# A two-layer decoder trunk: products taken in pairs at five places, and the remaining late transposes moved from TensorE to VectorE's blocks and DMAs

## The chip, the cores and the metric

The kernel runs on one core of one Trainium2 chip. The metric is the device time of one execution in microseconds (us), lower is better. The times shown are medians of several runs; the profile is one execution, with its own time beside them.

The core has five engines that run their own instruction queues in order and wait for each other by semaphores: TensorE (PE in the profile, its weight loads PEld), VectorE (DVE), ScalarE (ACT), GpSimd (POOL) and SyncE (SP). SP issues nearly all DMAs here. Matrix products are accumulated in PSUM, which has 8 banks of 128 x 512 float32; everything else is computed from SBUF, and HBM holds inputs, outputs and scratch.

## The reference

The reference is a trunk of two decoder layers over 256 tokens of width 2048, float32, causal. Layer 0 mixes tokens by softmax attention with 16 heads and a forget gate, layer 1 by a mixture of three dilated windows with 8 heads. Each mixer and each MLP follows an RMSNorm, and each adds into one residual stream.

```
for i in range(2):
    h = rms_norm(x, mix_norm_g[i])
    x = x + (fox_attention(h, ...) if i == 0 else dilated_attention(h, ...))
    h = rms_norm(x, mlp_norm_g[i])
    x = x + (relu(h @ mlp_w_up[i]) ** 2) @ mlp_w_down[i]

# fox_attention, per head: q, k are RMS-normalised per head
s = q @ k.T * dh ** -0.5 + c[q] - c[k]         # c: running sum of log forget gates
o = softmax(causal(s)) @ v                     # then o @ w_out

# dilated_attention, per head: three groups g with dilations r = 1, 4, 16, one shared v
s_g = q_g @ k_g.T * dh ** -0.5 - slope * distance   # only distances that r divides, up to 128 * r
o = softmax over all three groups together, @ v     # then o @ w_out
```

## The kernel before

**Products.** All large products run in float32 by splitting each operand into a rounded high part (`fp32r`) and a rest: high x high, high x low, low x high. Weights come from HBM in tiles of 256 rows by 512 columns (`load`, line 262, 512 KB, five buffers `raw`), in the order of the list `plan` (lines 213 to 241). `split` (line 282) makes the two parts: ScalarE casts the tile to `wh` (line 294), VectorE subtracts to `wl` (line 295; called the cut below), five buffers each.

A product has 512 output columns and 16 steps, one for each 128 rows of the contraction (`KC = 16`); every second step uses up one weight tile and calls `split` for the tile five further on. `product` (line 312) accumulates both 128-token halves in two PSUM banks (`acc`, 4 banks, so two products' worth), with six 128x512 matmuls in a step. `product_transposed` (line 359) is the MLP's up product with the weights stationary and the output transposed; it takes four banks: two of `acc` and two of either `sc` or `tp` (`up_banks`, line 861, alternating). The matmuls of one product follow step by step, and one product follows the other.

**The order of everything else.** The class `Jobs` (line 41) counts steps (`tick`). Chains of other work are generators: `yield 3` waits three steps, `yield key` waits until another chain has set that key, and `need(key)` makes a product wait for its input's key. So the numbers in the yields fix where a chain's instructions stand between the matmuls of the products; a scheduler then orders each engine's queue from that program. `behind(...)` asks that an instruction be put behind another one.

**Stages.** Norm n0 and the input; the first layer's queries, keys, values for four groups j of four heads (three products each, with the heads' attention in between); its output projection, four products; MLP n1 (four blocks of four up products and four down products); the dilated layer, four quarters q4 of three products for queries and keys (one for each dilation) and one for the shared values, with two heads each; its output projection; MLP n3.

**Transposes of the residual stream.** The stream `xt` is held token by token in four chunks of 512 columns. After the last product that adds to chunk n (`add_chain`, line 804), `norm_chain` (line 428) turns that chunk into `hT`, the stationary operand of the next stage, four of its 16 steps. For norms n1, n2, n3, chunks 0 to 2 go by `transposed_by_dma` (line 398): per 128 tokens one VectorE transpose in 32x32 blocks (line 405), four 64 KB DMAs into a scratch tensor in HBM (line 408) and one 256 KB DMA back (line 410), all on SP's queue; then ScalarE and VectorE make the two parts (lines 421, 422). The last chunk goes by eight 128x128 transposes on TensorE (line 440), since its product is the last ahead of the stage: only the 12 steps of chunks 0 to 2 stand between it and its use. Then the squares are summed (line 456) and `rstd` is made; it scales the results of the products, not their input.

**Heads.** `qk_chain` (line 482) takes a product of queries and/or keys: squares on ScalarE (line 488), sums on VectorE (line 492), a power on POOL (line 495), three steps later the scaling (lines 499, 501), VectorE's block transposes (line 533), four writes on SP (line 537) and a read on POOL (line 538) for each half, and after `yield 10` and two times `yield 2` the parts (lines 547 to 556). Two groups, named in `by_engine` (line 480), go by TensorE transposes (line 510) and are done sooner: the last keys of the first layer and the last group of the dilated layer, whose heads the output projection waits for. `v_chain` (line 559) takes the values. `fox_head` (line 699) and `dil_head` (line 750) compute a head: scores on TensorE (lines 708, 614, 617) into `sc` banks (two), mask and maximum on VectorE (716, 719; 763, 769), exponentials on ScalarE, scaling on VectorE (727; 777 to 780), three transposes of the probabilities on TensorE (`p_transposed`, line 588), and products with the values (`pv`, line 580). `gate_chain` (line 636) makes the running sum of the log forget gates; line 678 is its small matmul. `dilation_tables` (line 186) makes the distance tables on VectorE.

Of the kernel before, what the change touches and what calls it, by code (L numbers as in the profile page):

```python
# [17 lines left out]
P = 128  # L18
# [18 lines left out]
W_SUB = 2  # L37
RAW_SUB = 2


# [47 lines left out]
def trunk(ctx: ExitStack, tc, x, fox_w_in, fox_b_f, fox_q_gain, fox_k_gain, fox_w_out, dil_w_in,  # L88
# [126 lines left out]
    def add(w, rows, cols):  # L215

        for r in range(rows[0], rows[1], RAW_SUB * P):
            plan.append((w, r, cols))

    for j in range(4):  # L220
        for part in range(3):
            add(fox_w_in[0], (0, D), [(part * D + j * NC, NC)])
    for n in range(NX):
        add(fox_w_out[0], (0, D), [(n * NC, NC)])

    def add_mlp(l):
        for b in range(4):
            for n in range(4):
                add(mlp_w_up[l], (0, D), [(b * D + n * NC, NC)])
            for n in range(NX):  # L230
                add(mlp_w_down[l], (b * D, (b + 1) * D), [(n * NC, NC)])

    add_mlp(0)
    for q4 in range(4):
        for g in range(3):
            c = g * DH * P + q4 * 2 * P
            add(dil_w_in[0], (0, D), [(c, 2 * P), (3 * DH * P + c, 2 * P)])
        add(dil_w_in[0], (0, D), [(6 * DH * P + q4 * NC, NC)])
    for n in range(NX):
        add(dil_w_out[0], (0, D), [(n * NC, NC)])  # L240
    add_mlp(1)
# [69 lines left out]

    def product(keys, lhs, post):

        acc = [ps_acc.tile([P, NC], F32, tag="acc", name=f"acc{used[0]}_{t}") for t in range(NT)]
        for k in range(KC):
            jobs.need(keys(k))
            i = k % W_SUB
            hi, lo = (in_turn(w[:, i, :]) for w in splits[used[0]])
            ah, al = lhs(k)
            for t in range(NT):  # L320
                tok = slice(t * P, (t + 1) * P)
                first, last = k == 0, k == KC - 1
                nc.tensor.matmul(acc[t], ah[:, tok], hi, start=first, stop=False)  # L323
                nc.tensor.matmul(acc[t], ah[:, tok], lo, start=False, stop=False)  # L324
                issued["product"] = nc.tensor.matmul(acc[t], al[:, tok], hi, start=False, stop=last)  # L325
            if i == W_SUB - 1:
                used[0] += 1
                split()
            jobs.tick()
        jobs.spawn(post(acc))  # L330

    def last_product(keys, lhs, ready):
# [25 lines left out]

    def product_transposed(keys, both, banks, post):


        for k in range(KC):
            jobs.need(keys(k))
            i = k % W_SUB
            hi, lo = splits[used[0]]
            tokens = both(k)
            for b in range(NC // P):
                col = slice(b * P, (b + 1) * P)

                def main(first, last):  # L370
                    issued["product"] = nc.tensor.matmul(  # L371
                        banks[b], hi[:, i, col], in_turn(tokens.rearrange("p x s -> p (x s)"), P // 2), start=first, stop=last)

                def rest():
                    nc.tensor.matmul(banks[b][:, 0:S], lo[:, i, col], in_turn(tokens[:, 0, :], P // 2), start=False, stop=False)  # L375

                if k == 0:
                    main(True, False)
                    rest()
                else:  # L380
                    rest()
                    main(False, k == KC - 1)
            if i == W_SUB - 1:
                used[0] += 1
                split()
            jobs.tick()
        jobs.spawn(post(banks))

# [9 lines left out]
    def transposed_by_dma(tag, col, n):  # L398
# [3 lines left out]
        for t in range(NT):  # L402
# [8 lines left out]
            tiles.append(tile_)  # L411
        yield 7
        for half in range(2):
            pr = n * 2 + half
            both = act.tile([P, 2, 2, S], F32R, tag="hT", name=f"hT_{tag}_{pr}", bufs=KC // 2)
            for i in range(2):
                gc = gain[:, col + pr * 2 + i:col + pr * 2 + i + 1]
                for t in range(NT):
                    src = tiles[t].rearrange("p (i b r) -> p b i r", i=4, b=4)[:, half * 2 + i]
                    hi, lo = (both[:, i, x, t * P:(t + 1) * P].rearrange("p (i r) -> p i r", i=4) for x in range(2))  # L420
                    on_act = nc.scalar.activation(hi, src, AF.Copy, scale=gc)
                    on_dve = nc.vector.scalar_tensor_tensor(lo, src, gc, hi.bitcast(F32), ALU.mult, ALU.subtract)
            issued[tag, pr] = issued[tag] = on_act, on_dve
# [4 lines left out]
    def norm_chain(tag, col, n, ssp, wait, later):  # L428
        yield wait
        if tag != "n0" and n < NX - 1:  # L430
            yield from transposed_by_dma(tag, col, n)
# [46 lines left out]


    by_engine = {("fk", 3), ("dqk", 3, 2)}  # L480

    def qk_chain(acc, tag, key, parts):
# [15 lines left out]
        for t in range(NT):  # L498
# [5 lines left out]
            qn.append(q)  # L504
        if key in by_engine:
            yield 4
            for t in range(NT):
                pt = ps_tp.tile([P, 4, P], F32, tag="tp", name=f"ptq_{key}_{t}")
                for h in range(4):
                    nc.tensor.transpose(pt[:, h, :], qn[t][:, h, :], ident)  # L510
                for c, nh, gcol, (whole, hi, lo) in parts:
                    src = pt[:, c // P:c // P + nh, :]
                    gc = gain[:, gcol:gcol + 1]
                    keys = hi.shape[2] == S
                    if t == 0:
                        nc.scalar.activation(whole, src, AF.Copy, scale=gc)
                        if not keys:
                            continue
                    at = slice(t * P, (t + 1) * P) if keys else slice(0, P)
                    for i in range(nh):  # L520

                        order = [x.rearrange("p (h n) -> p h n", h=2) for x in (hi[:, i, at], lo[:, i, at])]
                        of = src[:, i, :].rearrange("p (n h) -> p h n" if keys else "p (h n) -> p h n", h=2)
                        nc.scalar.activation(order[0], of, AF.Copy, scale=gc)
                        nc.vector.scalar_tensor_tensor(order[1], of, gc, order[0].bitcast(F32), ALU.mult, ALU.subtract)
                yield 1
            jobs.done.add(key)
            return

# [106 lines left out]
    def gate_chain(tag, pf):  # L636
# [38 lines left out]
        nc.vector.scalar_tensor_tensor(lf, s, -2.0, z, ALU.mult, ALU.add)  # L675
        yield 6
        pc = ps_sc.tile([P, NT, FH], F32, tag="sc", name="pc")
# [21 lines left out]
    def fox_head(j, hh, qT, kT, vt, sel):  # L699
# [4 lines left out]
        yield "mask"  # L704
        yield (2 if ("fk", j) in by_engine else 4) * hh + 2
        ps = ps_sc.tile([P, 512], F32, tag="sc", name=f"sc_f{h}")
# [23 lines left out]
        yield ("fv", j)  # L730
        yield 2
        if ("f", h // 2) not in oT:
# [17 lines left out]
    def dil_head(q4, i, qTs, kTs, vt):  # L750
        h = 2 * q4 + i
        for g in range(3):
            yield ("dqk", q4, g)
        yield (4 if ("dqk", q4, 2) in by_engine else 6) * i + 2
        s = work.tile([P, 3, 3 * P], F32, tag="sd", name=f"sd{h}", bufs=1)
# [34 lines left out]
    def dilated(tag):  # L790
        for q4 in range(4):
            qTs = [heads_pair(f"dqT{q4}_{g}", g, False) for g in range(3)]
            kTs = [heads_pair(f"dkT{q4}_{g}", 3 + g, True) for g in range(3)]
            for g in range(3):
                product(keys_h(tag), lhs_h(tag),
                        lambda acc: qk_chain(acc, tag, ("dqk", q4, g),
                                             [(0, 2, DIL_G + g, qTs[g]), (2 * P, 2, DIL_G + 3 + g, kTs[g])]))
            vt = values(f"dv{q4}")
            for i in range(2):
                jobs.spawn(dil_head(q4, i, qTs, kTs, vt))  # L800
            product(keys_h(tag), lhs_h(tag), lambda acc: v_chain(acc, tag, ("dv", q4), vt))

# [23 lines left out]

    def out_proj(keys, lhs, then=None, ready=None, scale=None):
        for n in range(NX):
            if ready is not None and n == NX - 1:
                last_product(keys, lhs, final_add(n, scale))  # L830
                continue
            product(keys, lhs, lambda acc, n=n: add_chain(acc, n, then, ready, scale))

# [33 lines left out]
    def mlp(tag, **after):  # L867
        for b in range(4):
            key = f"{tag}a{b}"
            aT = {}  # L870
            for n in range(4):
                product_transposed(keys_h(tag), lambda k: hT[tag][k // 2][:, k % 2], up_banks(key, n),
                                   lambda banks, n=n: up_chain(banks, key, n, aT))
            out_proj(lambda k: (key, k // 2),
# [42 lines left out]
    for j in range(4):  # L917
# [12 lines left out]
        for hh in range(4):  # L930
# [4 lines left out]
             lambda k: (oT["f", k // 2][0][:, k % 2, :], oT["f", k // 2][1][:, k % 2, :]),  # L935
             normed("n1", MLP_G))
    jobs.spawn(dilation_tables())
# [3 lines left out]
             lambda k: (oT["d", k // 2][0][:, k % 2, :], oT["d", k // 2][1][:, k % 2, :]),  # L941
             normed("n3", MLP_G + KC))
    mlp("n3", ready=store)
# [31 lines left out]
```

## Time and profile before

| | us |
|---|---|
| median of 3 runs (lowest, highest) | 2167.12 (2166.98, 2168.76) |
| the profiled execution | 2165.63 |
| its span, first to last instruction | 2163.9 |
| TensorE busy | 2151.7 |
| VectorE busy | 1396.2 |
| ScalarE busy | 1109.2 |
| POOL busy | 71.9 |
| span of the output projection of layer 0, about | 310 to 382 |
| MLP n1, about | 382 to 1055 |
| dilated layer, about | 1055 to 1420 |
| its output projection, about | 1420 to 1495 |
| MLP n3, about | 1495 to 2164 |

The granted TensorE clock is 1.0 throughout. The DMA engines are busy 66% of the time on the queue of the weights. In the profile's rows, matmuls are pipelined: the length of one (0.38 us for 128x512) is longer than the distance to the next one's start (0.216 us), and it is the distance that adds up to the span. A row "A <- B: total, times, longest" of the waits says that A's line stood idle until B's line had released it.

### The profile page before, as it was taken

The page shows a single profiled execution, that of the slowest core. Times are in us where ns is not written, and L with a number is a line of the kernel's source. Part 1 is how long each engine was busy: PE and PEld are TensorE (multiplying, and loading weights), DVE is VectorE, ACT ScalarE, POOL GpSimd, SP SyncE. Part 2 cuts the span into 40 slices and gives each one's busy share as a digit, 9 for nine tenths or more (in the row PEclk, how much of TensorE's full clock was granted, in tenths as well). Part 3 has the DMA queues.
Part 4 walks back from the last instruction along what each step waited for, and adds up shares of the span by engine and source line. Part 5 has one row for each costly group of instructions (what it writes and reads, how often), then busy time and mean ns, then how long its engine had stood idle before and what let it go on. Part 6 is the DMA issues. An engine that isn't in the chain of part 4 may idle for free.

```text
span 2163.9 us, 30015 instructions
## 1 busy us (share of the span) xinstructions
PE 2151.7 (99%) x11248; PEld 1917.1 (89%) x11248; DVE 1396.2 (65%) x1847; ACT 1109.2 (51%) x1536; POOL 71.9 (3%) x88
## 2 busy tenths in 40 slices
PE   9999999999999999999999999999999999999999
PEld 7888888998998998998888888888988988988988
DVE  6777796655665565566667777766655655655664
ACT  6565565544444454455555555655544544544442
POOL 1111000000000000000010010000000000000000
PEclk9999999999999999999999999999999999999999
DMA  7676658666666766767686776767666666666764
GB/s 250 220 224 187 223 176 262 200 201 203 202 203 201 201 203 204 200 200 243 216 254 202 243 224 196 238 202 240 203 202 201 201 204 203 199 202 204 202 210 143
DMA packets 285411, 454.11 MB, mean 210 GB/s; under 512 B 21144, under 2 KB 98512, under 8 KB 285264
## 3 DMA queue, kind: packets, MB, share of 16 engines
q1 hardware_dynamic: 281792, 442.08, 65.7%
q0 software_dynamic: 2912, 9.46, 1.2%
q8 instruction: 88, 1.44, 0.3%
q10 hardware_dynamic: 560, 0.66, 0.1%
q14 instruction: 59, 0.48, 0.1%
HBM read 435.86 MB, written 16.25 MB: 209 GB/s over the span
## 4 chain that ended last, share of the span: by engine, by line
PE 97%; DVE 1%; ACT 1%; issue 1%; POOL 0%; DMA 0%; ACTq 0%; POOLq 0%
PE acc L323 21%; PE acc L324 21%; PE acc L325 21%; PE up_n3a_acc L371 5%; PE up_n1a_acc L371 5%; PE up_n3a_sc L371 3%; PE up_n3a_tp L371 3%; PE up_n1a_tp L371 3%; PE up_n1a_sc L371 3%; PE up_n1a_acc L375 3%; PE up_n3a_acc L375 3%; PE up_n1a_sc L375 1%; PE up_n1a_tp L375 1%; PE up_n3a_sc L375 1%; PE up_n3a_tp L375 1%; DVE wl L295 1%
## 5 line engine op out<-in xcount | busy, mean ns | idle before, releaser
L295 DVE TENSOR_TENSOR wl<-raw,wh 128x1024 fp32r<-128x1024 f32 (+1 forms) x801 | 976.6, 1222 | 691.1 <-ACT wh L294 687.9
L294 ACT CAST wh<-raw 128x1024 fp32r<-128x1024 f32 (+1 forms) x801 | 838.5, 1047 | 926.5 <-PE acc L325 590.7
L323 PE MATMUL acc<-wh,hT_n 128*128 128x512 f32 x896 | 343.6, 384 | 0.2 <-ACT wh L294 0.2
L324 PE MATMUL acc<-wl,hT_n 128*128 128x512 f32 x896 | 340.3, 380 | 0.1
L325 PE MATMUL acc<-wh,hT_n 128*128 128x512 f32 x896 | 339.6, 379 | 0.0
L323 PE MATMUL acc<-wh,aTh_n1a 128*128 128x512 f32 x512 | 194.0, 379 | 0.0
L324 PE MATMUL acc<-wl,aTh_n1a 128*128 128x512 f32 x512 | 194.0, 379 | 0.0
L325 PE MATMUL acc<-wh,aTl_n1a 128*128 128x512 f32 x512 | 194.0, 379 | 0.0
L325 PEld LDWEIGHTS acc<-wh,hT_n 128*128 128x128 f32 x896 | 169.6, 189 | 24.1
L323 PEld LDWEIGHTS acc<-wh,hT_n 128*128 128x128 f32 x896 | 169.6, 189 | 22.7 <-ACT wh L294 0.6
L324 PEld LDWEIGHTS acc<-wl,hT_n 128*128 128x128 f32 x896 | 169.9, 190 | 22.2 <-DVE wl L295 0.4
L323 PE MATMUL acc<-wh,aTh_n3a 128*128 128x512 f32 x480 | 181.9, 379 | 0.0
L324 PE MATMUL acc<-wl,aTh_n3a 128*128 128x512 f32 x480 | 181.9, 379 | 0.0
L325 PE MATMUL acc<-wh,aTl_n3a 128*128 128x512 f32 x480 | 181.9, 379 | 0.0
L371 PE MATMUL up_n3a_acc<-hT_n,wh 128*128 128x512 f32 x512 | 181.6, 382 | 0.0
L371 PE MATMUL up_n1a_acc<-hT_n,wh 128*128 128x512 f32 x512 | 181.6, 382 | 0.0
L375 PE MATMUL up_n1a_acc<-hT_n,wl 128*128 128x256 f32 x512 | 139.6, 273 | 0.0
L375 PE MATMUL up_n3a_acc<-hT_n,wl 128*128 128x256 f32 x512 | 139.6, 273 | 0.0
L324 PEld LDWEIGHTS acc<-wl,aTh_n1a 128*128 128x128 f32 x512 | 96.8, 189 | 13.7
L325 PEld LDWEIGHTS acc<-wh,aTl_n1a 128*128 128x128 f32 x512 | 96.8, 189 | 13.7
L323 PEld LDWEIGHTS acc<-wh,aTh_n1a 128*128 128x128 f32 x512 | 96.8, 189 | 13.7
L371 PEld LDWEIGHTS up_n1a_acc<-hT_n,wh 128*128 128x128 f32 x512 | 96.8, 189 | 13.5
(729 smaller groups left out, 3207.0 us busy)
## 6 DMA issues: line engine op xcount, KB each, us to landing
raw<-in_mlp_w_up_dram SPq DMA_DIRECT2D x256, 512.0 KB, 4.0
raw<-in_mlp_w_down_dram SPq DMA_DIRECT2D x256, 512.0 KB, 3.8
raw<-in_dil_w_in_dram SPq DMA_DIRECT2D x192, 256.0 KB, 3.3
raw<-in_fox_w_in_dram SPq DMA_DIRECT2D x95, 512.0 KB, 4.2
raw<-in_fox_w_out_dram SPq DMA_DIRECT2D x32, 512.0 KB, 4.2
raw<-in_dil_w_in_dram SPq DMA_DIRECT2D x32, 512.0 KB, 7.0
raw<-in_dil_w_out_dram SPq DMA_DIRECT2D x32, 512.0 KB, 5.0
blocks_n<-turned_n SPq DMA_DIRECT2D x72, 64.0 KB, 2.1
```

What stands on the lines that cost most here:

```text
L294: issued["cast"] = nc.scalar.copy(hi[:, part, :], raw[:, part, :])
L295: issued["cut"] = nc.vector.tensor_sub(lo[:, part, :], raw[:, part, :], hi[:, part, :].bitcast(F32))
L323: nc.tensor.matmul(acc[t], ah[:, tok], hi, start=first, stop=False)
L324: nc.tensor.matmul(acc[t], ah[:, tok], lo, start=False, stop=False)
L325: issued["product"] = nc.tensor.matmul(acc[t], al[:, tok], hi, start=False, stop=last)
L371: issued["product"] = nc.tensor.matmul(banks[b], hi[:, i, col], in_turn(tokens.rearrange("p x s -> p (x s)"), P // 2), start=first, stop=last)
L375: nc.tensor.matmul(banks[b][:, 0:S], lo[:, i, col], in_turn(tokens[:, 0, :], P // 2), start=False, stop=False)
```

## The change

**Pairs.** At five places two products that follow each other are taken together: the first 12 steps of the first, the first 12 of the second, the last 4 of the first, the last 4 of the second (`CUT = 12`). The places are the first two products of both output projections, the first two up products of both MLPs, and the first two products of the dilated layer. `plan` is reordered in the same way, so the weights come in that order. `product` and `product_transposed` are split into a part that makes the banks and a part that runs given steps.

**Order in the dilated layer.** In the first quarter the values' product comes first, paired with that of the first dilation's heads; then the other two dilations. In the other quarters it stays last.

**Transposes.** The last chunk of n1, n2, n3 goes by `transposed_by_dma` as well, whose wait becomes 9 steps instead of 7 and whose parts are put behind the latest cast and cut; `by_engine` and its branch are gone, so all heads go by blocks and DMAs. n0 keeps TensorE.

**Waits.** In `gate_chain` 10 steps instead of 6 ahead of the running sum; in `fox_head` 3 steps instead of 2 between the transposes of the probabilities and the products with the values; the heads of the last group of the first layer stand 3 steps apart (2 before), the two heads of the last quarter of the dilated layer 6 apart (4 before).

```diff
+    def add_pair(*chunks):
+        for rows in ((0, CUT * P), (CUT * P, D)):
+            for w, cols in chunks:
+                add(w, rows, cols)
...
+    def in_pair(new, steps, posts):
+        banks = []
+        for n in range(2):
+            banks.append(new(n))
+            steps(banks[n], range(CUT))
+        for n in range(2):
+            steps(banks[n], range(CUT, KC))
+            jobs.spawn(posts[n](banks[n]))
...
-        yield 7
+        yield 9
...
-                    on_act = nc.scalar.activation(hi, src, AF.Copy, scale=gc)
-                    on_dve = nc.vector.scalar_tensor_tensor(lo, src, gc, hi.bitcast(F32), ALU.mult, ALU.subtract)
+                    with behind(issued["cast"]):
+                        on_act = nc.scalar.activation(hi, src, AF.Copy, scale=gc)
+                    with behind(issued["cut"]):
+                        on_dve = nc.vector.scalar_tensor_tensor(lo, src, gc, hi.bitcast(F32), ALU.mult, ALU.subtract)
...
-        if tag != "n0" and n < NX - 1:
+        if tag != "n0":
             yield from transposed_by_dma(tag, col, n)
...
-    by_engine = {("fk", 3), ("dqk", 3, 2)}
...
-        if key in by_engine:
-            yield 4
-            for t in range(NT):
-                pt = ps_tp.tile([P, 4, P], F32, tag="tp", name=f"ptq_{key}_{t}")
-                for h in range(4):
-                    nc.tensor.transpose(pt[:, h, :], qn[t][:, h, :], ident)
...
-        yield 6
+        yield 10
         pc = ps_sc.tile([P, NT, FH], F32, tag="sc", name="pc")
...
-        yield (2 if ("fk", j) in by_engine else 4) * hh + 2
+        yield (3 if j == 3 else 4) * hh + 2
...
         yield ("fv", j)
-        yield 2
+        yield 3
...
-        yield (4 if ("dqk", q4, 2) in by_engine else 6) * i + 2
+        yield 6 * i + 2
...
+            if q4 == 0:
+                in_pair(lambda n: sums(), lambda acc, ks: product_steps(acc, keys_h(tag), lhs_h(tag), ks),
+                        [value_post, heads_post(0)])
+            for g in range(1 if q4 == 0 else 0, 3):
+                product(keys_h(tag), lhs_h(tag), heads_post(g))
             for i in range(2):
                 jobs.spawn(dil_head(q4, i, qTs, kTs, vt))
-            product(keys_h(tag), lhs_h(tag), lambda acc: v_chain(acc, tag, ("dv", q4), vt))
+            if q4:
+                product(keys_h(tag), lhs_h(tag), value_post)
...
+        if pair:
+            in_pair(lambda n: sums(), lambda acc, ks: product_steps(acc, keys, lhs, ks), posts)
+        for n in range(2 if pair else 0, NX):
...
+            if b == 0:
+                in_pair(lambda n: up_banks(key, n), steps, posts)
+            for n in range(0 if b else 2, 4):
+                banks = up_banks(key, n)
+                steps(banks, range(KC))
+                jobs.spawn(posts[n](banks))
```

## The prediction

> **What bounds the kernel now.** I read the page first (shares, chain), then the waits of TensorE, then its rows in order of time at the places that the change touches, and last VectorE's rows there.
>
> ```profile
> PE 2151.7 (99%) x11248; PEld 1917.1 (89%) x11248; DVE 1396.2 (65%) x1847; ACT 1109.2 (51%) x1536; POOL 71.9 (3%) x88
> ...
> PE 97%; DVE 1%; ACT 1%; issue 1%; POOL 0%; DMA 0%; ACTq 0%; POOLq 0%
> ...
> PE po_f L580 <- DVE pTl_f L593: 2.2, 3, 0.7
> PE pc L678 <- DVE g_lf L675: 1.1, 1, 1.1
> PE sc_d L614 <- DVE sd L763: 0.2, 1, 0.2
> ```
>
> TensorE is the bound from end to end. After the first 15 us it waits measurably five times in 2150 us. So only two things pay: fewer matmuls on it, and those five waits; anything new that makes it wait is lost in full. The unit below is the step (one of 16 in a product): six 128x512 matmuls, 0.216 us from start to start, 1.29 us.
>
> ```profile
> 383.52 0.38 PE L371 MATMUL up_n1a_sc<-hT_n,wh 128*128 128x512 f32 x1
> ...
> 384.73 0.60 PE L440 MATMUL ptx_n<-ident,x 128*128 128x128 f32 x4
> ...
> 385.27 0.38 PE L371 MATMUL up_n1a_sc<-hT_n,wh 128*128 128x512 f32 x1
> ...
> 401.76 0.38 PE L371 MATMUL up_n1a_sc<-hT_n,wh 128*128 128x512 f32 x1
> ...
> 403.07 0.38 PE L371 MATMUL up_n1a_sc<-hT_n,wh 128*128 128x512 f32 x1
> ...
> 115.82 0.27 PE L580 MATMUL po_f<-pTh_f,fv0h 128*128 128x256 f32 x1
> 116.82 0.38 PE L580 MATMUL po_f<-pTl_f,fv0h 128*128 128x256 f32 x1 [0.73 <-DVE pTl_f L593]
> ```
>
> The columns are start, length, engine, line, tile. A step of the up product takes 403.07 - 401.76 = 1.31 us, and one with four transposes in it 385.27 - 383.52 = 1.75 us. The last two rows start 1.00 us apart where such rows elsewhere start 0.11 apart: one of three equal waits.
>
> **The change, part by part.**
>
> *Transposes removed.* The last chunk of norms n1, n2, n3 (8 each) and the two groups in `by_engine` (8 each): 40, in ten groups of four. 10 x (1.75 - 1.31) = -4.4 us, all of it on the bounding engine. The Trainium skill ("TensorE: Matmul & The Clock Gate", Part 4: PE-mode transpose) gives about 275 ns for one in a kernel; 40 of those are an estimated 11.0 us, and the time by that would be 2155.9. The row here is as long (0.28 us), but they overlap: four move the next matmul by 0.44 us, so the trace's 4.4 stands.
>
> *What replaces them.* Per chunk two VectorE transposes (0.70 us each), eight 64 KB writes and two 256 KB reads on SP's queue; for the two head groups also, with the reads on POOL's. In sum 5 x 10 = 50 DMAs more, 46 on SP, 4 on POOL. The three chunks have cover: their first use is 24 steps (31 us) after the product that makes them, against 12 before, and chunks 0 to 2 take the same way in the kernel before without a wait on TensorE. Without that cover the path would show: in the kernel before, from the first write (322.88) to the landing of the second read (330.86 + 3.7) it is 11.7 us. The two head groups finish 17 steps after their product (yields of 3, 10, 2 and 2), their last head 35 steps after it, and the pair needs the last heads 40 steps after it (16 of the value product, 24 of the pair). Cost 0.
>
> *Waits moved.* `yield 3` puts the value products of a head (L580) one step, 1.29 us, later; the wait was 1.00 - 0.11 = 0.89 us, three times: -2.7. The wait before L614 at 1406 us (0.37 us by starts) came from the two heads standing four steps apart; they go back to six, as in the three earlier quarters, which show none: -0.4. The gate's cumulative sum (L678) started 1.49 us after the matmul ahead of it, where 0.22 is usual: 1.27 us. In the built order it stands one step later, 1.29 us, which just covers that; but the transposes of its result (L685) now wait for a copy that stands behind a cut (1.23 us) and a reduction (0.6) on VectorE, until about 63.4 us where TensorE is there at 63.1: +0.3. Net -1.0.
>
> *Pairs.* Both need accumulators at once: 4 banks, or all 8 in the up product. The third product of a stage starts only 4 steps (5.2 us) after the first of the pair ends, and takes its banks. Up: in the kernel before, the last bank is read out at 406.9 for a product that ended at 403.9, 3.0 us. Output projection: two adds (1.28 us) and a cut. Dilated: v_chain, about 2.2 us. All under 5.2: cost 0, and what is above it would be paid at each of five places.
>
> *The value product first.* In the first quarter of the dilated layer the three head products now end the quarter, so head 0's scores meet the norm chain of the next quarter's first heads, which they did not before. This is the one new wait I can place. The chain without a collision, and the head without one:
>
> ```profile
> 1119.22 0.36 DVE L499 TENSOR_SCALAR rq_('dqk', 0, 2)_10200<-rq_('dqk', 0, 2)_10200,rstd_n 128x4 f32<-128x4 f32 x2 [1.54 <-POOL rq_('dqk', 0, 2)_10200 L495]
> 1119.49 0.69 DVE L501 TENSOR_TENSOR qn_('dqk', 0, 2)_0_10238<-acc,rq_('dqk', 0, 2)_10200 128x512 f32<-128x512 f32 x1
> 1120.10 1.22 DVE L295 TENSOR_TENSOR wl<-raw,wh 128x1024 fp32r<-128x1024 f32 x1
> 1121.23 0.68 DVE L501 TENSOR_TENSOR qn_('dqk', 0, 2)_1_10241<-acc,rq_('dqk', 0, 2)_10200 128x512 f32<-128x512 f32 x1
> ...
> 1137.51 0.38 PE L614 MATMUL sc_d<-dkT_0w,dqT_0w 128*128 128x128 f32 x2
> ...
> 1141.21 0.38 PE L614 MATMUL sc_d<-dkT_2w,dqT_2w 128*128 128x128 f32 x2
> ...
> 1148.80 0.49 PE L588 MATMUL ptp_d<-ident,p_d 128*128 128x128 f32 x3
> ...
> 1139.46 1.21 DVE L763 SCALAR_TENSOR_TENSOR sd<-dist,sc_d 128x384 f32<-128x384 f32 x2
> ...
> 1142.56 1.41 DVE L769 TENSOR_REDUCE nm_d<-sd 128x1 f32<-128x384 f32 x2
> ```
>
> The third head product ends 19 steps before the first scores: 1137.51 - 24.58 = 1112.93. Counted from a product's end, VectorE is held by the power on POOL until 6.3 us, does L499 and L501, a cut, and is free at 8.3. In the changed order the first L763 stands there, ahead of the second L501; it ends at 8.9. TensorE issues the scores of the three dilations at 3.9, 5.7 and 7.6 (three steps in, 1.85 us apart); the third takes the first one's bank of the two, so it waits 8.9 - 7.6 = +1.3. Then VectorE does the second L501, two transposes and a cut (0.6 + 0.6 + 0.6 + 1.1) before the other two L763 (1.2): 12.9. L769 to 14.35, the exponentials to 15.4, reciprocal and two adds to 16.6, a cut to 17.75, the first scaling to 18.1. The transposes L588 would stand at 1148.80 - 1112.93 - 20.70 = 15.2, with the first wait at 16.5: +1.6. Head 1's L588 then meets the end of that chain: three more casts on ScalarE (1.5 us) and a subtraction on VectorE (0.48) ahead of the values' operands, which had 0.2 us to spare: +0.8. Together +3.7; from below 0 (VectorE gets ahead after all), from above 7, if both heads wait as long.
>
> Sum: -4.4 - 2.7 - 0.4 - 1.0 + 3.7 = -4.8 us; I take -4.6, since a step or two of rounding in the hidden places is more likely lost than won. The profiled execution has a span of 2163.9 us and a time of 2165.6; the median of the runs is 2167.1, 1.5 above it. I put the difference on the median: **2162.5 us**.
>
> **The rivals.**
>
> *No collision (2158.8).* VectorE finds the scores earlier than I place them and the 3.7 us do not appear. For it: VectorE idles 35% of the span, and L593 has met such chains with waits of only 0.89 us. Against it: two of the three waits follow from the order of one queue. 2162.5 - 3.7.
>
> *Further waits eat the rest (2165 to 2168).* The mechanism is VectorE's in-order queue at the other new seams: the four last heads of the first layer at three steps with some 20 operations of the distance tables between them (my count leaves 0.6 us for the last one), and the third product's banks with 2 us to spare at five places. 0.5 to 1 us at six such places gives 3 to 6: 2165.5 to 2168.5. For it: the three waits of L580 show how little it takes. Against it: in the kernel before heads stand two steps apart among the same table operations with no wait.
>
> *Weights late, slower (2175).* In the two paired output projections chunks 0 and 1 end 5.2 us apart, and 17 small DMAs stand in a row on SP ahead of the next weight tile; before it was nine, and weights resumed 4.35 us after the first write (327.23 - 322.88). Now I count 5.3 us until chunk 1 can be written, then eight writes of 0.42, two reads of 0.34 and 0.8 of waiting for a landing: 10.2. The tile delayed first is used 18 steps (23.3 us) after chunk 0 ends; with 2.3 us for adds and transpose ahead of the first write, 10.2, 4.2 for landing and 2.3 for cast and cut, 4.3 us are left. Past that every microsecond is paid, twice. If the run lasts 21 us (ten landings of 2.1 us one after another), it is 2 x 6.5 = 13: 2175.5. For it: SP issues in order and the reads wait for landings. Against it: two landings wait together, and the DMA engines are 66% busy. The Trainium skill ("VectorE: DVE Perf Modes", Rules for kernel authors) sends a full 128x128 transpose to TensorE where PSUM may take it; by that rule this change goes the wrong way. The trace agrees on the length of the path (11.7 us against 0.44), not on who pays for it.
>
> That the transposes stay is no rival: the built order has none of the 40.
>
> **How the numbers follow.** Forecast 50% (spread 2161 to 2165), no collision 17%, further waits 22%, weights late 11%. Runs of this kernel tell 0.2% (4.3 us) from no change, so faster means under 2162.8: 29 points of the forecast and the 17, 46%. Within 0.2%: the other 21 and the 22, 43%. Slower: 11%. The range 2158.3 to 2168.5 holds all but the last and a tail.
>
> **What would show it.** Right: no rows of the transposes in norms n1 to n3; no waits of L580's and L614's old places; a wait of the scores of 1 to 2 us and one of L588's successor of 1 to 2 us some 30 us into the dilated layer's second quarter, and nowhere else above 0.5. Wrong: TensorE waiting for the casts of weights in an output projection (third rival), for banks in the third product of a pair (second), or no wait of the scores at all (first).

## The result, and the profile after

| | before | after |
|---|---|---|
| median of 11 runs each, us | 2166.88 (2166.04 to 2168.76) | 2162.35 (2160.25 to 2163.88) |
| ratio, 95% interval | | 0.9976 [0.9968, 0.9984] |
| profiled execution, us | 2165.63, span 2163.9 | 2161.91, span 2160.2 |
| first matmul's start to last one's end, us | 2157.51 | 2154.17 |
| of it the plain distances of all matmuls, us | 2141.14 | 2136.70 |
| of it everything else, us | 16.37 | 17.48 |

The last two rows are made from TensorE's rows: each matmul's distance to the next is compared with the median distance for its shape; the medians sum to the first, what is above them to the second. The change took 4.44 us of matmuls away, and TensorE waits 1.1 us longer than before. So five waits were removed, 4.3 us in all, and more than they were worth came back.

From the page of the changed kernel: the shares, and the chain that ended last.

```profile
PE 2147.8 (99%) x11208; PEld 1912.6 (89%) x11208; DVE 1397.9 (65%) x1862; ACT 1105.9 (51%) x1545; POOL 74.1 (3%) x92
...
PE 92%; DVE 3%; DMA 2%; issue 1%; ACT 1%; POOL 0%; SPq 0%; DVEq 0%; ACTq 0%; POOLq 0%
```

40 instructions fewer on TensorE, 15 more on VectorE. The chain now leaves TensorE for 8% of the span where it was 3%. That share is not time lost, for TensorE is still busy for 99%: from each wait of TensorE the chain is followed back through the work that released it, often for tens of us. Where time is lost, the waits of TensorE tell (released by; total, times, longest, in us):

```profile
PE sc_d L620 <- DVE sd L769: 1.3, 2, 0.7
PE sc_f L623 <- ACT fkT_0h L560: 1.1, 1, 1.1
PE ptp_d L594 <- DVE p_d L786: 1.0, 1, 1.0
```

None of these four waits was there before (the one wait of the first kind that was, 0.2 us at 1406 us, is gone); the waits of the value products and of the gate are gone too. (New line numbers: L614, L617, L588 before are L620, L623, L594 now; L763, L769 are L769, L775; L501 is L531; L678 is L684.) In order of time on TensorE:

```profile
85.43 0.38 PE L620 MATMUL sc_f<-fkT_0w,fqT_0w 128*128 128x128 f32 x2
86.96 0.38 PE L623 MATMUL sc_f<-fkT_0h,fqT_0h 128*128 128x256 f32 x1 [1.15 <-ACT fkT_0h L560]
87.43 0.38 PE L623 MATMUL sc_f<-fkT_0l,fqT_0h 128*128 128x256 f32 x1
...
1157.28 0.46 PE L620 MATMUL sc_d<-dkT_2w,dqT_2w 128*128 128x128 f32 x2 [0.65 <-DVE sd L769]
...
1166.12 0.70 PE L594 MATMUL ptp_d<-ident,p_d 128*128 128x128 f32 x3 [1.01 <-DVE p_d L786]
...
1228.49 0.46 PE L620 MATMUL sc_d<-dkT_2w,dqT_2w 128*128 128x128 f32 x2 [0.64 <-DVE sd L769]
```

By distances of starts these are 1.32 + 0.36 us at 87 us (the first head of the first layer), 0.82 at 1157, 1.18 at 1166, 0.80 at 1228, and small ones behind them. The second and third are the seam that the prediction placed, where the heads of the dilated layer's first quarter meet the next quarter's chain; the first and the last it did not have. The first has its cause on ScalarE and GpSimd:

```profile
73.19 0.53 POOL L747 MEMSET self<- 128x512 f32 x1 [8.08 <-DVE fqT_1l L562]
73.80 2.54 POOL L749 TENSOR_SCALAR_AFFINE_SELECT self<-self 128x512 f32<-128x512 f32 x2
76.29 0.60 POOL L544 DMA_DIRECT2D qn_('fk', 0)_0_771<-blocks_('fk', 0)_0_777  x1
```

```profile
81.91 0.51 ACT L553 ACTIVATE fkT_0w<-qn_('fk', 0)_0_771,gain 128x256 f32<-128x256 f32 x1 [1.87 <-DMA qn_('fk', 0)_0_771<-blocks_('fk', 0)_0_777]
...
86.50 0.41 ACT L560 CAST fkT_0h<-sq_('fk', 0)_0_715 128x256 fp32r<-128x256 f32 x1
86.81 0.42 ACT L560 CAST fkT_1h<-sq_('fk', 0)_0_715 128x256 fp32r<-128x256 f32 x1
87.12 1.05 ACT L308 CAST wh<-raw 128x1024 fp32r<-128x1024 f32 x1
```

GpSimd builds the next group's selector (L747, L749, 3.1 us) and only then issues the read of the first keys, at 76.29. ScalarE waits 1.87 us for that read and casts until 87.2. The same place in the kernel before:

```profile
85.87 0.51 ACT L554 CAST fkT_0h<-sq_('fk', 0)_0_732 128x256 fp32r<-128x256 f32 x1
...
86.79 0.38 PE L614 MATMUL sc_f<-fkT_0w,fqT_0w 128*128 128x128 f32 x2
86.93 0.36 PE L617 MATMUL sc_f<-fkT_0h,fqT_0h 128*128 128x256 f32 x1
```

There the cast that TensorE needs next (fkT_0h) ended at 86.38, and TensorE came to L617 at 86.93 with 0.55 us to spare. Now the cast ends 0.53 us later (86.91), and TensorE comes to the scores 1.36 us earlier (85.43 against 86.79), because it no longer stands 1.27 us before the gate's sum. The greater part of the gate's wait was not removed, it was passed on.

VectorE at the seam of the dilated layer, in order:

```profile
1155.46 1.22 DVE L309 TENSOR_TENSOR wl<-raw,wh 128x1024 fp32r<-128x1024 f32 x1
1156.59 0.55 DVE L769 SCALAR_TENSOR_TENSOR sd<-dist,sc_d 128x384 f32<-128x384 f32 x1
1157.06 0.68 DVE L531 TENSOR_TENSOR qn_('dqk', 1, 0)_1_10644<-acc,rq_('dqk', 1, 0)_10598 128x512 f32<-128x512 f32 x1
1157.66 0.70 DVE L539 STREAM_TRANSPOSE sq_('dqk', 1, 0)_0_10590<-qn_('dqk', 1, 0)_0_10641 128x512 f32<-128x512 f32 x1
1158.28 0.67 DVE L539 STREAM_TRANSPOSE sq_('dqk', 1, 0)_1_10592<-qn_('dqk', 1, 0)_1_10644 128x512 f32<-128x512 f32 x1
1158.87 1.18 DVE L309 TENSOR_TENSOR wl<-raw,wh 128x1024 fp32r<-128x1024 f32 x1
1159.98 1.00 DVE L769 SCALAR_TENSOR_TENSOR sd<-dist,sc_d 128x384 f32<-128x384 f32 x2
```

The head's first L769 stands behind a cut of weights (L309), the other two behind the next quarter's scaling, its two transposes and another cut: the order that the prediction wrote down. The third scores start 0.1 us after the first L769 ends (1157.14), since they take its bank.

### The profile page after: what moved, and what is told of

The parts are those of the page before. It is cut to its first block, busy times and chain, and to the rows that moved or that the text cites. A ratio compares the mean times of both kernels' runs of the same rounds, so it can differ in the third digit from the quotient of the medians.

```text
span 2160.2 us, 30057 instructions
## 1 busy us (share of the span) xinstructions
PE 2147.8 (99%) x11208; PEld 1912.6 (89%) x11208; DVE 1397.9 (65%) x1862; ACT 1105.9 (51%) x1545; POOL 74.1 (3%) x92
## 4 chain that ended last, share of the span: by engine, by line
PE 92%; DVE 3%; DMA 2%; issue 1%; ACT 1%; POOL 0%; SPq 0%; DVEq 0%; ACTq 0%; POOLq 0%
PE acc L340 19%; PE acc L341 19%; PE acc L339 19%; PE up_n1a_acc L403 5%; PE up_n3a_acc L403 5%; PE up_n3a_sc L403 3%; PE up_n1a_tp L403 3%; PE up_n1a_sc L403 3%; PE up_n3a_tp L403 3%; PE up_n3a_acc L407 3%; PE up_n1a_acc L407 3%; DMA raw<-in_dil_w_in_dram 2%; DVE wl L309 1%; PE up_n3a_tp L407 1%; PE up_n1a_sc L407 1%; PE up_n1a_tp L407 1%
## 5 line engine op out<-in xcount | busy, mean ns | idle before, releaser
L309 DVE TENSOR_TENSOR wl<-raw,wh 128x1024 fp32r<-128x1024 f32 (+1 forms) x801 | 975.0, 1221 | 686.7 <-ACT wh L308 681.0
L403 PEld LDWEIGHTS up_n3a_acc<-hT_n,wh 128*128 128x128 f32 x512 | 96.8, 189 | 13.5
```

The costliest lines, as they stand in the source:

```text
L309: issued["cut"] = nc.vector.tensor_sub(lo[:, part, :], raw[:, part, :], hi[:, part, :].bitcast(F32))
L403: issued["product"] = nc.tensor.matmul(banks[b], hi[:, i, col], in_turn(tokens.rearrange("p x s -> p (x s)"), P // 2), start=first, stop=last)
```

## The experiments

Twelve kernels, all with runs of the kernel before beside them on the same chip; its medians there were 2167.08, 2166.91, 2166.79 and 2166.14 us in the four sets, so a time is read against its own set where tenths matter.

**The seam, moved away.**

```diff
-        yield 6 * i + 2
+        yield 6 * i + (5 if q4 == 0 else 2)
```

> The changed kernel with one number different: the two heads of the dilated layer's first quarter start five steps after their last chain instead of two (3.9 us later). Theory (the heads' scores meet the next quarter's first norm chain on VectorE): the waits of 0.8 us at the third scores, 1.2 us at the transposes of the probabilities and 0.2 to 0.3 us at head 1, all between 1157 and 1181 us, go, nothing takes their place: 2162.35 - 2.2 = about 2160.1 us. Rival (the waits come with the new order of products, from banks or from ScalarE, wherever the heads stand): they move along by 3.9 us and the time stays at 2162.3 +- 0.5. The waits of 0.8 and 0.3 us at 1228 and 1236 us stay in both, if they belong to the program (a weight tile that lands late behind the eight writes of a chain), and are missing here if they were an accident of one execution.

2159.43 us (2158.52 to 2160.19), ratio 0.9965 [0.9952, 0.9977]; all five runs are below the lowest of the changed kernel. Waits of TensorE in its profile:

```profile
PE sc_f L623 <- ACT fkT_0h L560: 1.3, 1, 1.3
PE ptp_d L594 <- DVE p_d L786: 0.4, 1, 0.4
```

No wait of the dilated layer's scores is left. Between 1150 and 1200 us TensorE's excess over plain distances falls from 2.93 to 1.36 us (0.09 in the kernel before): the collision is the cause, and three steps undo somewhat over half of it, 1.57 us where I had expected 2.2. The largest pieces of the rest are 0.28 us at head 0's transposes and 0.52 at head 1's. The waits at 1228 and 1236 us (1.3 us of excess there in the changed kernel's profile) are missing too, though nothing was changed there.

**The gate, put back.**

```diff
-        yield 10
+        yield 6
         pc = ps_sc.tile([P, NT, FH], F32, tag="sc", name="pc")
```

> The changed kernel with the gate's cumulative sum four steps earlier again (six steps, as before the change). Theory (what the later gate won, 1.27 us at 61 us, is given back by the first heads' scores, which now come 1.3 us earlier than the keys are ready, 1.32 + 0.36 = 1.68 us at 87 us): the wait at 61 us is back, the one at 87 us is gone or under 0.4 us, and the time is 2162.0, within 0.5 of the changed kernel. Rival (the prediction's step: the later gate is worth 1.0 us net): 2163.4 us, and a wait at 87 us that stays.

2160.98 us (2160.10 to 2163.47), ratio 0.9974 [0.9963, 0.9986], against 0.9976 for the changed kernel: no loss from taking back what was to win 1.0 us, though by the times alone the rival's 2163.4 (0.9983 of this set's before) lies just inside the interval. The rows decide (the first line is the gate's wait):

```profile
PE pc L684 <- DVE g_lf L681: 1.1, 1, 1.1
PE ptp_d L594 <- DVE p_d L786: 1.0, 1, 1.0
PE sc_d L620 <- DVE sd L769: 0.6, 1, 0.6
```

By starts 1.27 us is back at 61 us, and at 87 us nothing above 0.15 is left of 1.68. So the later gate costs 0.4 us in these rows. What it loses at 87 us differs between executions, from 1.02 to 1.84 us in the seven profiles that have the late gate and GpSimd's old order; against a gain of 1.27 us that is nothing won, give or take half a us. The median is 1.0 us under the 2162.0 that I expected: the rest of the difference to the changed kernel's profile is once more the waits at 1228 and 1236 us, which are absent.

**The read let past the selector.**

```diff
-        sel = make_sel(j)
+        sel = make_sel(j) if j == 0 else None
...
+        sel = sel or make_sel(j)
         for hh in range(4):
             jobs.spawn(fox_head(j, hh, qT, kT, vt, sel))
```

> The changed kernel with the selector of the head groups 1 to 3 built behind the group's second product instead of ahead of its first, so that GpSimd does not fill and select (3.1 us) ahead of the first read of the first keys at 76 us. Theory (that read is what makes the keys late): the read is issued about 2 us earlier, the wait of 1.32 + 0.36 us at 87 us goes, and the time is 2162.35 - 1.7 = 2160.7 us. Rival (the keys are late because VectorE turns them later, behind the gate's copies, or because the scores simply come earlier): the second read sets the end, the wait stays above 1 us and the time at 2162.3 +- 0.5.

2159.96 us (2158.28 to 2160.97), ratio 0.9967 [0.9954, 0.9979]. The read, the last cast and the scores:

```profile
73.40 0.58 POOL L544 DMA_DIRECT2D qn_('fk', 0)_0_771<-blocks_('fk', 0)_0_777  x1 [8.48 <-DVE fqT_1l L562]
...
84.97 0.49 ACT L560 CAST fkT_1h<-sq_('fk', 0)_0_715 128x256 fp32r<-128x256 f32 x1
...
85.23 0.38 PE L620 MATMUL sc_f<-fkT_0w,fqT_0w 128*128 128x128 f32 x2
85.37 0.36 PE L623 MATMUL sc_f<-fkT_0h,fqT_0h 128*128 128x256 f32 x1
```

The read goes out 2.9 us earlier, and L623 follows L620 after 0.14 us. That GpSimd's order made the keys late is shown; with it mended, no wait stands at 61 us nor at 87 us, so by the rows the later gate is worth its 1.27 us.

**The pairs undone.**

```diff
-        for rows in ((0, CUT * P), (CUT * P, D)):
-            for w, cols in chunks:
-                add(w, rows, cols)
+        for w, cols in chunks:
+            add(w, (0, D), cols)
...
         for n in range(2):
-            banks.append(new(n))
-            steps(banks[n], range(CUT))
-        for n in range(2):
-            steps(banks[n], range(CUT, KC))
-            jobs.spawn(posts[n](banks[n]))
+            banks = new(n)
+            steps(banks, range(KC))
+            jobs.spawn(posts[n](banks))
```

> The changed kernel with the five pairs undone: products one after the other, whole, in the same order; all later transposes still go by blocks and DMAs. Theory (the pairs are the cover of the DMA path: without them the last chunk is used 12 steps, 15.5 us, after it is made, where the path takes some 2.3 + 10.2 + 4.2 + 2.3 = 19 us, and the last heads of a layer are used 31 and 28 steps after their product where they need 35): waits of about 3.5 us at each of the three norms and of 4 to 6 us at each of the two output projections, 2162.35 + 20 = 2182 us, between 2172 and 2192. Rival (the path is short enough, and the pairs cost or win nothing): 2161.5 to 2163.5 us.

2165.05 us (2164.02 to 2167.76), ratio 0.9993 [0.9984, 1.0002]. A miss by 17 us: the pairs are worth 2.7 us by the medians, not 20. TensorE's new waits are 1.50 us at norm n3's last chunk and 0.33 at n1's; small ones sum to 0.4 at n2's and to 1.0 and 0.6 at the two output projections. That is 4 us, and the waits at 1228 and 1236 us are absent here. The longest new one, with ScalarE's row that ends it:

```profile
1507.33 0.27 PE L403 MATMUL up_n3a_tp<-hT_n,wl 128*128 128x256 f32 x1
...
1508.49 2.16 ACT L449 ACTIVATE hT_n<-turned_n,gain 128x128 fp32r<-128x128 f32 x7 [1.07 <-DMA turned_n<-blocks_n]
...
1508.94 0.49 PE L403 MATMUL up_n3a_sc<-hT_n,wl 128*128 128x256 f32 x2 [1.34 <-ACT hT_n L449]
```

The path from a product's end to the operand took 15.5 + 1.5 = 17.0 us here and 15.8 at n1, where I had 19. For the heads I had counted steps: what is left of their chain when TensorE gets there is issued at once, and takes far less than the steps that it was spread over.

The seam's 2.93 us of excess is in this profile too: it comes with the order of the products, not with the pairing. By these rows the pair of the dilated layer covers 0.4 us, and the order that was changed for it costs 2.8. No run here puts that order alone back.

**The transposes put back**, with pairs and steps as in the changed kernel (`n < NX - 1` and `by_engine` as before):

> The changed kernel with its pairs and steps, but with the 40 transposes on TensorE again (the last chunk of three norms, the two last head groups), and without the 50 DMAs that took their place. Theory (those transposes cost their place in the queue of matmuls and nothing else; the DMAs that replace them are hidden): the plain distances of the matmuls sum to 2141.1 us again instead of 2136.7, and the time is 2162.35 + 4.4 = 2166.8 us, between 2165.5 and 2167.5. Rival (the replacement loads VectorE, ScalarE and SP and costs part of the gain elsewhere): less than +3 us, under 2165.3. Rival by a page's figure (some 275 ns for one transpose): 2173 us.

2166.40 us (2165.56 to 2173.41), ratio 1.0002 [0.9993, 1.0011]. The plain distances sum to 2141.14 again. TensorE waits in one new place by more than 0.3 us, 0.85 us at 385 us, where the transposes come ahead of the sum that they read. The theory holds. The rival by the figure on "TensorE: Matmul & The Clock Gate" in the Trainium skill (Part 4: PE-mode transpose, about 275 ns each) does not: a row of such a transpose is as long as that, but 40 of them are worth 4.4 us of time, not 11.

**The value products put back.**

```diff
         yield ("fv", j)
-        yield 3
+        yield 2
         if ("f", h // 2) not in oT:
```

> The changed kernel with the value products of the first layer's heads one step earlier again, as before the change. Theory: the three waits of 0.89 us at 116, 186 and 256 us are back and nothing else moves: 2162.35 + 2.7 = 2165.0 us. Rival (each is a wait that another would take up, as the gate's was): under +1.3 us, below 2163.7.

2165.16 us (2163.45 to 2167.41), ratio 0.9992 [0.9983, 1.0001]. `PE po_f L586 <- DVE pTl_f L599: 2.2, 3, 0.7` is in its waits again; by starts 0.888, 0.887 and 0.891 us, the size and the places of before. The wait at 87 us is 0.66 + 0.36 us in this execution.

**Only the two numbers**, in the kernel before (value products 2 to 3, gate 6 to 10):

> The kernel before with two numbers of the change alone: the heads' value products one step later and the gate's sum four steps later; no pair, no other transposes. Theory (the first wins 2.67 us of three waits; the second wins 1.27 us at 61 us and loses 1.1 to 1.7 us at 87 us): 2166.9 - 2.7 + 0.1 = 2164.3 us. Rival (the prediction's steps: -2.7 - 1.0): 2163.2 us. Second rival (the three waits need the pairs' order to stay away): over 2165.5 us.

2163.80 us (2162.81 to 2164.88), ratio 0.9985 [0.9976, 0.9993]. Its waits, with L614 and L617 as in the kernel before:

```profile
PE sc_f L617 <- ACT fkT_0h L554: 0.5, 1, 0.5
PE sc_d L614 <- DVE sd L763: 0.2, 1, 0.2
```

The three waits and the gate's are gone, 0.67 + 0.36 us stand at 87 us, and the second line is the old wait of 1406 us (at 1404 here), 0.376 us by starts, where the two heads still stand four steps apart. The time lies between theory (2164.3) and rival (2163.2), nearer the first. Two thirds of the change's 4.5 us are had without a pair or a DMA; the rest of it, 4.4 us of transposes less some 2.8 at the seam, adds 1.5.

**Both waits treated**: the edits of the later seam and the later selector.

> The changed kernel with both edits of the runs before together: the selector built later, and the heads of the dilated layer's first quarter three steps later. Theory (the two waits are independent, 1.7 us at 87 us and about 1.6 us net between 1157 and 1181 us): 2159.96 - 1.6 to 2.2 = about 2158.0 us, with 0.4 to 0.5 us left at the two heads' transposes of the probabilities at 1168 and 1180 us. Rival (the later selector shifts VectorE's work of the first layer alone, and what the dilated seam won is bounded by the accident of a late weight tile): no better than 2159.5 us.

2158.49 us (2156.99 to 2159.34), ratio 0.9961 [0.9948, 0.9973]. By the rows the two are independent: nothing above 0.21 us stands at 87 us, and 1.10 us of excess between 1150 and 1200. The times alone don't tell, since the rival's 2159.5 (0.9966 of this set's before) lies inside the interval. In this profile a wait of 0.75 + 0.29 us stands at 1404 and 1412 us, at the same scores of the fourth quarter where the changed kernel had them in the second.

**One step more**: `6 if q4 == 0` for `5`.

> As the run before, with the heads of that quarter four steps later instead of three. Theory (the rest of the collision moves with the place: one more step puts head 0's scores wholly behind the chain of the next quarter's first heads): the 0.4 us at 1168 us goes, and the time is 0.3 to 0.8 us below three steps, about 2157.5 us. Rival (head 1 then meets the chain of the quarter's second heads): a wait of about 1 us at a new place, 2158.5 us or more.

2159.18 us (2158.75 to 2160.20), ratio 0.9966 [0.9953, 0.9978]: the rival. Head 0's wait is gone, and head 1's transposes wait 1.75 us at 1180 us; 0.42 + 0.29 us stand at 1226 and 1234. By the times of five runs each the two versions can't be told apart.

**Weights: the writes on GpSimd**, in the version with both waits treated.

```diff
-                nc.sync.dma_start(blocks[:, :, i, :]...
+                (nc.gpsimd if tag == "n2" else nc.sync).dma_start(blocks[:, :, i, :]...
```

> The version with both waits treated, with the eight block writes of each head chain of the dilated layer issued by GpSimd instead of SP, so that no weight tile stands behind them. Theory (the waits of 0.4 to 0.8 us that appear in some executions at the third scores of a later quarter, 1404 us in the last version, 1228 us in the changed kernel, come from a weight tile that is issued behind a chain's writes and lands 2 us late): none of them in the profile, no cast of the dilated layer that waits over 1 us for a weight tile's landing, and the time is 2157.0 us, its runs within 1.5 us. Rival (the tile is late for the memory's sake, not the queue's, or the wait is VectorE's order alone): such waits still appear, 2158.5 +- 0.5. Price that may come instead: GpSimd's issue takes 0.55 us each, and a chain's reads then land later; if past their cover, waits of the first scores of a quarter by 1 us or more, over 2161 us.

2189.27 us (2189.16 to 2191.83), ratio 1.0106 [1.0093, 1.012]. The named price came, and it is so large that the run says nothing on the weights. In order on GpSimd:

```profile
1142.84 1.63 POOL L543 DMA_DIRECT2D ks_('dqk', 0, 2)_1_10453<-sq_('dqk', 0, 2)_1_10377  x3
1146.13 0.57 POOL L544 DMA_DIRECT2D qn_('dqk', 0, 2)_0_10440<-ks_('dqk', 0, 2)_0_10446  x1 [1.66 <-DMA ks_('dqk', 0, 2)_0_10446<-sq_('dqk', 0, 2)_0_10375]
1146.69 0.56 POOL L543 DMA_DIRECT2D ks_('dqk', 0, 2)_1_10453<-sq_('dqk', 0, 2)_1_10377  x1
1152.78 0.56 POOL L544 DMA_DIRECT2D qn_('dqk', 0, 2)_1_10443<-ks_('dqk', 0, 2)_1_10453  x1 [5.53 <-DMA ks_('dqk', 0, 2)_1_10453<-sq_('dqk', 0, 2)_1_10377]
```

The last write stands behind a read that waits for landings, the second read then waits another 5.5 us for that write's landing, and goes out at 1152.78 (1142.51 with the writes on SP). The third dilation's scores of each quarter's first head then wait 6.6, 2.2, 6.7 and 7.2 us; they take the bank of the first dilation's scores, and VectorE's L769, which frees it, stands behind the late chain.

**Weights: two more raw tiles**, first in the version with both waits treated, then in the changed kernel alone.

```diff
-RAW_BUFS = 5
-W_BUFS = 5
+RAW_BUFS = 7
+W_BUFS = 4
```

> The version with both waits treated, with seven raw weight tiles and four pairs of split ones instead of five and five: the loads run one tile (2.6 us) further ahead of use, the casts one tile less. Theory (weights that land late are the rest of the dilated layer's waits): as by the writes on GpSimd, 2157.0 us. Rival (it is the casts' distance that gives cover to VectorE and ScalarE): waits of TensorE for casts appear wherever chains crowd the two engines, over 2160 us.

2157.53 us (2156.91 to 2158.33), ratio 0.9958 [0.9944, 0.9971]: the lowest median of all, though its runs overlap those of the version without (2156.99 to 2159.34). No wait of the dilated layer's scores is in its profile in any quarter.

> The changed kernel with seven raw weight tiles and four pairs of split ones, and nothing else. Theory (the waits of 0.8 and 0.3 us at 1228 and 1236 us, in the changed kernel's profile and in no other with the same dilated layer, are weight tiles that land late in some executions, and make its runs spread from 2160.3 to 2163.9): they are absent, the waits at 87 us (1.3 to 1.8 in sum) and between 1157 and 1181 us (2.9) stay, the median is 2161.2 us and the runs lie within 2 us. Rival (the spread and the wait have another cause): 2162.3 us and a spread of over 3 us.

2161.21 us (2160.15 to 2163.04), ratio 0.9978 [0.9968, 0.9988]. The waits at 1228 and 1236 us are absent, those at 87 us (1.62) and between 1150 and 1200 us (2.93) stay, as expected. But one run of nine is at 2163.04, a spread of 2.9, and the kernel before was 0.7 us lower in this set: the ratio is no better than the changed kernel's. That weights which land late make the spread is not shown.

What is shown of them is ScalarE's rows of the changed kernel ahead of the wait at 1228 us:

```profile
1217.82 1.05 ACT L308 CAST wh<-raw 128x1024 fp32r<-128x1024 f32 x1 [1.65 <-DMA raw<-in_dil_w_in_dram]
...
1222.54 1.04 ACT L308 CAST wh<-raw 128x1024 fp32r<-128x1024 f32 x1 [1.70 <-DMA raw<-in_dil_w_in_dram]
```

The second cast waits for a weight tile's landing, what follows it on ScalarE and VectorE slips, and L769 comes late for the third scores' bank. Of the seven profiles whose heads stand as in the changed kernel, only its own has this wait, so it belongs to an execution and not to the program. What makes the tile late is not shown.

## Why the prediction was right, point by point

2162.5 against 2162.35. The direction and the main gains were right, but that the number came so close is luck: three terms of the sum were off, by +1.4, -0.9 and +1.4 us in these rows, and cancelled only in part. The rows of the two profiled executions differ by 2.9 us where the sum had 4.8, their spans by 3.7, and the medians by 4.5.

| term | predicted, us | rows, us |
|---|---|---|
| 40 transposes | -4.4 | -4.44 |
| value products a step later | -2.7 | -2.67 |
| heads six steps apart | -0.4 | -0.37 |
| later gate | -1.0 | -1.27 + 1.68 = +0.4 |
| collision at the seam | +3.7 | +2.8 (2.93 - 0.09) |
| later quarters | 0 | +1.4 (1.44 - 0.08, from 1200 to 1250 us) |

The rows sum to -2.9; pieces under 0.2 us spread over the span make it the -3.3 from first to last matmul, and the last store, which ends 0.3 us sooner behind the last matmul, the -3.7 of the span.

- *Transposes removed*: right in size and kind; with them back (the experiment) the sum of distances is the old one to 0.01 us. Their DMAs are hidden, as costed. The cover named for it was too pessimistic: without the pairs 2.7 us come back.
- *Waits moved*: `yield 3` and the old wait at 1406 us right to 0.03 us. **The step that failed is the gate's**: "In the built order it stands one step later, 1.29 us, which just covers that; but the transposes of its result (L685) now wait for a copy". I looked for what is late next on VectorE and found a wait that did not come: the copy stood behind the cut and the reduction as written, but ended at 63.26 us, and TensorE came at 63.46. What was late next was on TensorE's own path: everything behind the gate comes 1.3 us earlier, up to the first scores, whose keys do not: their cast ended at 86.38 in the kernel before, at 86.91 in the changed one and at 86.88 with the gate put back. In the kernel before, TensorE was there 0.55 us behind the cast, and the profile had no wait to show it. Putting the gate back and letting the read past the selector, each alone, show both halves of this.
- *The value product first*: the place, the order on VectorE and the three waits were right, the size 0.9 too large. The third scores waited 0.82 us for 1.3, the transposes 1.18 + 0.15 for 1.6, head 1 some 0.55 in four pieces, at the value products and not at its transposes, for 0.8; the rest of the 2.8 is pieces under 0.15. That it is the collision is shown by the later heads.
- *Pairs' banks at 0*: right; no third product of a pair waits.
- *Rivals*: no collision (2158.8) fell in the profile; its price of 3.7 us was too high, since the rows put the whole seam at 2.8. The version with the later heads runs at 2159.4, but it still has 1.3 us of the seam and lacks the waits at 1228 and 1236 us. Weights late in the paired output projections (2175.5) did not occur: TensorE shows no wait of 0.15 us or more in either. Further waits did occur, 1.7 + 1.4 us in two places that I had not named, inside that rival's price but not by its mechanism: the first is a cast of ScalarE behind GpSimd's late read, the second follows a weight tile that landed late in one execution. The time stayed at the forecast all the same, since the gains were right, the seam was over-priced, and the second of these waits is absent from the six other profiles with the same heads.

## What to carry to other kernels

When a wait on the bounding engine is removed, go forward on that engine to the next consumer of something another engine delivers at a fixed time, and compare the two times there: the profile of before shows no wait at a place that is reached just in time (here with 0.55 us to spare). A transpose among other matmuls is worth its place in the queue, not its length in the row, so moving it to DMAs pays that little and no more; the cheap edits (one step in a schedule, the order on a queue that looks idle) were worth as much here: 3.0 us for two numbers, by the rows nearly all of it the value products' step, and 1.7 by its rows for a selector built later, where the exchange of the transposes won 4.4 us and its new order lost 2.8 of them again.

## What the runs showed of the hardware

After a long wait TensorE runs at half its clock. In the version with the writes on GpSimd (stretch and its length, busy time of PE, PEld, DVE, ACT, POOL, granted clock, DMA share, GB/s):

```profile
1165.50:1169.00 3.50, 3.47 (x11) 3.04 (x12) 3.50 (x5) 0.00 (x0) 2.13 (x4) 0.50 0.89 278
...
1235.40:1239.00 3.60, 3.53 (x11) 3.11 (x12) 3.40 (x5) 0.71 (x2) 0.00 (x0) 0.53 0.69 214
1239.00:1243.00 4.00, 4.00 (x20) 3.49 (x20) 2.38 (x5) 3.03 (x4) 0.00 (x0) 1.00 0.27 79
```

For 3.4 to 5.2 us behind each of its four long waits, 128x512 matmuls start 0.427 us apart instead of 0.216: 1.9 to 2.7 us more for a wait. Waits of 1.0 us here and of 1.75 us in the version with heads four steps later had no such tail; one of 2.2 us had. The Trainium skill ("TensorE: Matmul & The Clock Gate", Part 1: The HAM clock gate) says that the clock falls to half after an idle window of some 3.4 us and rises again after a busy one of that length. The half rate agrees with it, and so does the shortest tail; but a wait of 2.2 us, shorter than that window, was enough to set it off here.

The other surprise is how unequal two ways to issue the same write are: in the first two chains of the dilated layer 64 KB from SP landed in 1.7 to 2.2 us (the version with both waits treated), from GpSimd in 2.6 for the first four of a chain and 4.5 to 4.9 for the last four (medians of four each).
